# Two-layer encoder trunk: half-width products that take all of k, heads kept in memory, sums on GpSimd

## The chip, the cores and the metric

The kernel runs on one core of one Trainium2 chip. The core's engines are TensorE (PE in the profile: the matrix products; PEld are its weight loads), VectorE (DVE), ScalarE (ACT) and GpSimd (POOL); SyncE (SP) issues most transfers between the chip's memory and SBUF. Each engine works through a list of instructions of its own, in order, and waits at an instruction until what it needs is there. The metric is the device time of one execution in microseconds (us).

## The reference

```python
def reference(x, mem, norm_g, w_in, na_rpb, mem_norm_g, w_mem_kv, w_out, final_g):
    ...
    for l in range(DEPTH):
        h = rms_norm(x, norm_g[l])
        z = h @ w_in[l]
        na_q, na_k, na_v, na_g, dl_q, dl_k, dl_v, dl_g, m_q, m_g = jnp.split(z, offsets, axis=-1)
        ...
        y = jnp.concatenate([o_na * jax.nn.silu(na_g), o_dl * jax.nn.silu(dl_g), o_m * jax.nn.silu(m_g)], axis=-1)
        x = x + y @ w_out[l]
    return rms_norm(x, final_g)
```

Two layers over 512 tokens of 2048 channels in fp32. One projection feeds 16 attention heads of 128 channels (6 neighbourhood, 6 dilated, 4 memory heads) and 16 gates; each head's output times its SiLU gate is one of 16 column tiles of `y`, and a second projection of 16 column tiles is added to `x`.

## The kernel before

Activations lie transposed: a tile has 128 channels on the partitions and 512 tokens along the free side, so `act` (the input of a layer) and `mix` (the gated heads) are 16 tiles each, one for each k tile of the products after them. An fp32 operand is split into a rounded high part and a low remainder (`split`: a ScalarE copy, then a VectorE subtraction), and one product is three matmuls on these parts (`mm3`). Weights come from memory in halves of 8 k tiles (128x1024), are split likewise (`wr` raw, `wh` high, `wl` low; four buffers of each), and `next_half` prepares three halves ahead of the one in use.

A layer runs its value, query and key projections with the attention of each head threaded between them (`steps`, `pump`), then 16 gate columns, then 16 output columns. A plain column (`gemm_t`) is 48 matmuls of 512 tokens. Pairs of columns (`gemm_two`) use a two-by-two scheme of seven products for eight: weights a1, a2 (first column, lower and upper k) and b1, b2 (second column), and tokens cut into a left and a right half of 256. Sums of weights (`combine`, L210 to L213, VectorE) and sums of activations (`whole` and `mix_pair`, L310 to L325, VectorE) are made beside. Before the change a pair takes that scheme on 4 pairs of k tiles, and 8 of the 16 k tiles run plain at 512 tokens (`plain`): 48 matmuls of 512 and 84 of 256. Gate columns 4 to 13 and output columns 2 to 15 (2 to 13 in the second layer, whose last two are done in token halves for the final norm) are such pairs: 23 pairs and 16 plain columns in all.

A head's output stays in SBUF (`o`), and is multiplied by its gate there (L648); the 16 splits of the gated heads (L669) stand between the gates and the output columns. Tiles come from tagged pools, of which the change uses: `u` (63 buffers), `p` (4: scores of a head, old values, sums), `pth` and `ptl` (2 each), `tmp` (4). An instruction that writes a new tile waits until some buffer of its tag is free, that is, until the last reader of an older tile is done. A scheduler sets the order on each engine when the program is built.

Of the kernel before, what the change touches and what calls it, by code (L numbers as in the profile page):

```python
# [9 lines left out]
F32 = mybir.dt.float32  # L10
# [23 lines left out]
U_BUFS = 63  # L34
PAIRS = 4
PLAIN = 2
GATES = range(4, 14)
ASIDE = (2, 3)
# [41 lines left out]
def hybrid_kernel(ctx: ExitStack, tc: tile.TileContext, xT, memT, gains, rpbw, wts, cs_tab, dil_tab, na_tab, outT):  # L80
# [65 lines left out]
    for _ in range(WARM):  # L146
        nc.tensor.matmul(bank[:, :P], lhsT=ones, rhs=ones, start=True, stop=True)
    xs = dpool.tile([KO, P, T], F32, tag="xs", name="xs")


    stream = []
    for layer in range(NL):
        at = 0
        two_by_two = {"o": range(PLAIN, KO if layer + 1 < NL else KO - LAST), "g": GATES}
        for key in SEQ:
            tiles = 4 if key[0] in ("v", "mv") else 1
            if key[1] not in two_by_two.get(key[0], ()):
# [41 lines left out]
    def combine(layer, part, two, at=None):  # L199
# [4 lines left out]
        if part == "raw":  # L204
            a, b, s1 = f32t("wr", W_BUFS, W_HALF), f32t("wr", W_BUFS, W_HALF), tmp()
            two.update(a=a, b=b, s1=s1)
            nc.sync.dma_start(out=a, in_=wts[layer, at, :, :W_HALF])
            nc.sync.dma_start(out=b, in_=wts[layer, at + 1, :, :W_HALF])
# [658 lines left out]
```

## Time and profile before

| | us |
|---|---|
| median of 3 runs (1846.49 to 1846.89) | 1846.72 |
| profiled execution | 1847.28 |
| its span | 1845.5 |
| PE busy in it | 1831.0 (99%) |
| DVE busy | 1086.0 (59%) |
| ACT busy | 751.1 (41%) |
| POOL busy | 53.3 (3%) |

The span runs from the first to the last instruction; the rest of the execution's time lies around it. The granted TensorE clock is 0.998 of full speed (2.4 GHz) over the span. An engine's busy time counts from the start to the end of each instruction, with the time in which another engine holds it up inside it. Neighbouring VectorE instructions overlap a little in the records, so that starts tell better than durations what one costs.

### The profile page before, as it was taken

What the parts mean: (1) busy time and instruction counts of PE and PEld (TensorE: products, weight loads), DVE (VectorE), ACT (ScalarE), POOL (GpSimd) and SP (SyncE); (2) the same over time, 40 slices, a digit from 0 to 9 for tenths busy, and PEclk for the clock granted to TensorE, in tenths of its full rate; (3) what the DMA queues carried; (4) which work ended last, traced back from release to release, by engine and by line L of the source; (5) the groups of instructions that cost most, each with busy time, mean ns of one, the idle gap of its engine ahead of it and who ended that gap; (6) DMA issues with size and microseconds to landing.
All of it is one profiled execution on the core that took longest, in us unless ns stands there. A gap on an engine that the chain in (4) does not pass through costs nothing.

```text
span 1845.5 us, 24250 instructions
## 1 busy us (share of the span) xinstructions
PE 1831.0 (99%) x9586; PEld 1569.0 (85%) x9586; DVE 1086.0 (59%) x1803; ACT 751.1 (41%) x1188; POOL 53.3 (3%) x111
## 2 busy tenths in 40 slices
PE   9999999999999999999999999999999999999997
PEld 8888988888888898899888888888888888988987
DVE  7457553463566866666654564435636658676665
ACT  6346442333334434433443453323333444454442
POOL 0113000100000000000000100000000000000000
PEclk9999999999999999999999999999999999999999
DMA  7335423222222233344643353232222222333433
GB/s 283 102 102 156 137 69 98 89 75 86 86 78 81 79 98 121 123 140 160 183 149 96 112 172 114 70 102 81 69 91 80 78 71 80 104 120 115 132 107 110
DMA packets 69201, 202.99 MB, mean 110 GB/s; under 512 B 7264, under 2 KB 16992, under 8 KB 69088
## 3 DMA queue, kind: packets, MB, share of 16 engines
q1 hardware_dynamic: 68800, 201.16, 34.1%
q8 instruction: 75, 1.23, 0.3%
q10 hardware_dynamic: 288, 0.30, 0.1%
q14 instruction: 38, 0.31, 0.1%
HBM read 193.04 MB, written 8.39 MB: 109 GB/s over the span
## 4 chain that ended last, share of the span: by engine, by line
PE 97%; DVE 1%; DMA 0%; issue 0%; ACT 0%; ACTq 0%; DVEq 0%; SPq 0%
PE acc L247 80%; PE sc L247 10%; PE pv L247 4%; PE sc L418 2%; DVE u L228 0%; DVE wl L222 0%; PE acc L342 0%; DVE wr L761 0%; DMA g_sb<-in_gains 0%; DMA u<-in_memT 0%; PE sc L399 0%; PE sc L746 0%; PE sc L385 0%; DVE p L460 0%; ACT u L227 0%
## 5 line engine op out<-in xcount | busy, mean ns | idle before, releaser
L247 PE MATMUL acc<-u,wh 128*128 128x512 f32 (+1 forms) x3976 | 1113.2, 366 | 0.0
L247 PEld LDWEIGHTS acc<-u,wh 128*128 128x128 f32 x3976 | 706.7, 189 | 107.4
L247 PE MATMUL acc<-u,wl 128*128 128x512 f32 (+1 forms) x1988 | 724.7, 365 | 0.0
L222 DVE TENSOR_TENSOR wl<-wr,wh 128x1024 fp32r<-128x1024 f32 (+1 forms) x344 | 420.8, 1223 | 371.9 <-ACT wh L221 370.6
L221 ACT CAST wh<-wr 128x1024 fp32r<-128x1024 f32 (+1 forms) x344 | 360.6, 1048 | 541.4 <-PE acc L247 436.1
L247 PEld LDWEIGHTS acc<-u,wl 128*128 128x128 f32 x1988 | 375.2, 189 | 61.2
L247 PE MATMUL acc<-wh,u 128*128 128x512 f32 x880 | 283.0, 391 | 0.0
L247 PEld LDWEIGHTS acc<-wh,u 128*128 128x128 f32 x880 | 165.2, 188 | 33.7 <-DVE u L228 0.3
L247 PE MATMUL acc<-wl,u 128*128 128x512 f32 x440 | 171.5, 390 | 0.0
L247 PE MATMUL sc<-u,wh 128*128 128x256 f32 x736 | 138.3, 286 | 0.0
L222 DVE TENSOR_TENSOR ptl<-sc,pth 128x512 fp32r<-128x512 f32 (+2 forms) x112 | 67.5, 603 | 93.6 <-ACT pth L221 93.1
L247 PEld LDWEIGHTS sc<-u,wh 128*128 128x128 f32 x736 | 117.3, 191 | 5.2
L221 ACT CAST pth<-sc 128x512 fp32r<-128x512 f32 (+2 forms) x112 | 57.9, 517 | 123.3 <-PE sc L418 122.7
L247 PE MATMUL sc<-u,wl 128*128 128x256 f32 x368 | 104.1, 283 | 0.0
L247 PEld LDWEIGHTS acc<-wl,u 128*128 128x128 f32 x440 | 82.7, 188 | 16.2
L450 ACT ACTIVATE p<-p,stat 128x256 f32<-128x256 f32 (+1 forms) x96 | 59.2, 616 | 86.9 <-DVE stat L460 86.1
L247 PE MATMUL sc<-u,u 128*128 128x256 f32 (+1 forms) x384 | 80.5, 322 | 0.0
L247 PEld LDWEIGHTS sc<-u,u 128*128 128x128 f32 x384 | 65.3, 188 | 11.6
L247 PEld LDWEIGHTS sc<-u,wl 128*128 128x128 f32 x368 | 70.3, 191 | 0.0
L247 PE MATMUL pv<-pth,u 128*128 128x512 f32 (+2 forms) x224 | 68.4, 386 | 0.0
L221 ACT CAST u<-tmp 128x512 fp32r<-128x512 f32 (+1 forms) x64 | 37.9, 592 | 68.9 <-DVE tmp L580 67.2
L418 PEld LDWEIGHTS sc<-ident,p 128*128 128x128 f32 x376 | 47.8, 140 | 15.2 <-DVE p L453 0.6
(137 smaller groups left out, 1201.0 us busy)
## 6 DMA issues: line engine op xcount, KB each, us to landing
wr<-in_wts SPq DMA_DIRECT2D x319, 512.0 KB, 3.6
p<-in_xT SPq DMA_DIRECT2D x23, 256.0 KB, 4.8
p<-xs SPq DMA_DIRECT2D x22, 256.0 KB, 3.4
u<-in_memT SPq DMA_DIRECT2D x16, 256.0 KB, 4.3
xs<-u SPq DMA_DIRECT2D x16, 256.0 KB, 2.0
outT<-wr SPq DMA_DIRECT2D x6, 512.0 KB, 2.9
e<-in_rpbw SPq DMA_DIRECT2D x12, 192.0 KB, 2.4
pth<-in_xT SPq DMA_DIRECT2D x4, 256.0 KB, 4.9
```

The costliest lines, as they stand in the source:

```text
L221: nc.scalar.copy(hi, x)
L222: nc.vector.tensor_tensor(lo, x, hi.bitcast(F32), ALU.subtract)
L247: nc.tensor.matmul(out, lhsT=a[i], rhs=b[j], start=start and n == 0, stop=stop and n == 2, skip_group_check=shared)
L418: nc.tensor.transpose(tr[:, i * P:(i + 1) * P], probs[qt][:, col:col + P], ident)
L450: nc.scalar.activation(s, src, AF.Exp, bias=neg_max, scale=scale, accum_out=l)
```

## The change

- Pairs of the kind `ns == 8` take the scheme on all 8 pairs of k tiles: seven products of 24 matmuls of 256 tokens, and no plain part. Their weights come as four halves at once (b2, a1, a2, b1), and the four sums s1 = b1 + b2, s3 = b1 + a1, s2 = a1 + s1, s4 = a2 + s2 are made in place, 128x1024 each. Pairs of the kind `ns == 4` keep the old arithmetic.
- Gates: columns 2 to 5 are two pairs of 4, columns 6 to 13 four pairs of 8. Output: columns 2 and 3 a pair of 4, columns 4 to 13 five pairs of 8. In both layers; in all 6 pairs of 4, 18 pairs of 8 and 14 plain columns (the last two of layer two aside, as before).
- Every sum of weights (`add`) and of activations (`mix_pair`) is made by GpSimd. There are 8 sums of activations (`mixed`) for the gates and 8 for the output columns, in place of 4 and 4; each has five GpSimd instructions on 128x256.
- Each head's output goes to memory (`ys`) and is loaded again for its gate; the gated head goes back to `ys`. The splits for the output columns are spread over the last two gate columns (`next_mix`), and the sums for the output columns load their two heads into the two `ptl` buffers (`mix_heads`). Layer two's new columns go to memory (`zs`) and are loaded before the last two columns.
- Tables (mask and rotary) lie in `u` buffers, loaded in each layer; `u` has 66 buffers.

```text
ns == 8, order of the products: b2*mixed[2], a1*left, a2*left, s1*mixed[0], s2*mixed[1], s4*right, s3*mixed[3]
```

```diff
...
-PAIRS = 4
-PLAIN = 2
-GATES = range(4, 14)
-ASIDE = (2, 3)
+U_BUFS = 66
+
+
+GATES_TWO = {2: 4, 4: 4, 6: 8, 8: 8, 10: 8, 12: 8}
+OUT_TWO = {2: 4, 4: 8, 6: 8, 8: 8, 10: 8, 12: 8}
 LAST = 2
...
+        two_by_two = {"g": GATES_TWO, "o": OUT_TWO}
...
+            ns = [two_by_two.get(key[0], {}).get(j) for j in (key[1], key[1] - 1)]
+            if ns[0]:
+
+                two = {"at": at}
+                parts = ("b2", "a1", "a2", "s1", "s2", "s4", "s3") if ns[0] == 8 else (
+                    "first", "a1 a2", "second", "s2 s4", "s1", "s3 b2")
+                stream += [(layer, key, (part, two)) for part in parts]
+            elif not ns[1]:
...
+        def add(out, x, y):
+            nc.gpsimd.tensor_tensor(out, x, y, ALU.add)
...
+        if part in ("first", "second"):
+            return split(load(0 if part == "first" else 1, None, rest), hi, lo)
+        if part == "b2":
+            for name, i, h in (("b2", 1, 1), ("a1", 0, 0), ("a2", 0, 1), ("b1", 1, 0)):
+                two[name] = load(i, h, every)
+        if part == "a1 a2":
+            a, b, s1 = load(0, None, some), load(1, None, some), tmp()
+            two.update({"a1 a2": a, "s2 s4": a, "s3 b2": b, "s1": s1})
...
+            add(s1, b[:, :T], b[:, T:])
+            add(b[:, :T], b[:, :T], a[:, :T])
+            add(a[:, :T], a[:, :T], s1)
+            add(a[:, T:], a[:, T:], a[:, :T])
...
+        w = two[part]
+        n = w.shape[-1]
+        split(w, hi[:, :n], lo[:, :n])
+        if part == "a1":
+            two["s1"], two["s3"], two["s2"] = two["b2"], two["b1"], two["a1"]
+            add(two["s1"], two["b1"], two["b2"])
+            add(two["s3"], two["b1"], two["a1"])
+            add(two["s2"], two["a1"], two["s1"])
+        if part == "a2":
+            two["s4"] = two["a2"]
+            add(two["s4"], two["a2"], two["s2"])
+        return hi, lo
...
-                mm3(acc, (hi[:, sl], lo[:, sl]), act[8 + k8], k8 == 0, False)
+                mm3(acc, (hi[:, sl], lo[:, sl]), act[ns + k8 if k8 < 8 - ns else 8 + k8], k8 == 0, False)
...
-        def product(out, w, c0, b, start=False, stop=False, shared=False):
-            for i in range(PAIRS):
+        def product(out, w, b, start=False, stop=True, c0=0, shared=True):
+            for i in range(ns):
                 sl = slice(c0 + i * P, c0 + (i + 1) * P)
-                mm3(out, (w[0][:, sl], w[1][:, sl]), b(i), start and i == 0, stop and i == PAIRS - 1, shared=shared)
+                mm3(out, (w[0][:, sl], w[1][:, sl]), b(i), start and i == 0, stop and i == ns - 1, shared=shared)
...
+        product(second[:, left], weights(), mixed_of(2), start=True)
+        product(part[:, left], weights(), half_of(0, left), start=True)
         nc.scalar.copy(e1[:, left], part[:, left])
-        product(first[:, left], w, T, half_of(PAIRS, left))
-        plain(second)
-        w = next_half(l, key)
-        product(part[:, left], w, 0, mixed_of(1), stop=True, shared=True)
+        product(first[:, left], weights(), half_of(8, left), start=True)
+        product(part[:, right], weights(), mixed_of(0))
+        product(part[:, left], weights(), mixed_of(1))
         nc.scalar.copy(u2, part[:, left])
-        product(first[:, right], w, T, half_of(PAIRS, right), stop=True)
-        product(part[:, right], next_half(l, key), 0, mixed_of(0), stop=True, shared=True)
         nc.vector.tensor_tensor(e1[:, right], part[:, right], u2, ALU.add)
-        w = next_half(l, key)
-        product(part[:, left], w, 0, mixed_of(3), stop=True, shared=True)
+        product(first[:, right], weights(), half_of(8, right))
+        nc.vector.tensor_tensor(e1, first, e1, ALU.add)
+        product(part[:, left], weights(), mixed_of(3))
         nc.scalar.copy(e2[:, left], part[:, left])
-        nc.vector.tensor_tensor(e2[:, right], part[:, right], e2[:, left], ALU.add)
...
-        return (first, e1, ALU.add), (second, e2, ALU.subtract)
+        nc.vector.scalar_tensor_tensor(e2[:, right], part[:, right], -1.0, e2[:, left], ALU.mult, ALU.subtract)
+        nc.vector.tensor_tensor(e2[:, left], second[:, left], e2[:, left], ALU.subtract)
...
-        nc.vector.tensor_tensor(c[:, :n], y[:, :n], y[:, n:], ALU.subtract)
-        nc.vector.scalar_tensor_tensor(c[:, n:], c[:, :n], -1.0, z[:, n:], ALU.mult, ALU.subtract)
-        nc.vector.tensor_tensor(d[:, n:], z[:, n:], y[:, n:], ALU.subtract)
-        nc.vector.tensor_tensor(d[:, :n], z[:, :n], c[:, n:], ALU.add)
+        for out, a, b, op in ((c[:, n:], y[:, n:], y[:, :n], ALU.subtract), (c[:, n:], c[:, n:], z[:, n:], ALU.subtract),
+                              (c[:, :n], y[:, :n], y[:, n:], ALU.subtract), (d[:, n:], z[:, n:], y[:, n:], ALU.subtract),
+                              (d[:, :n], z[:, :n], c[:, n:], ALU.add)):
+            nc.gpsimd.tensor_tensor(out, a, b, op)
...
                 nc.scalar.copy(out[0], bank[0])
+                nc.scalar.dma_start(out=ys[MIX.index(name)], in_=out[0])
...
+        def head(j, tag="p"):
+
+            y = f32t(tag, 4 if tag == "p" else 2)
+            nc.sync.dma_start(out=y, in_=ys[j])
+            return y
+
+        def gate(j, z, y):
 
             e = tmp()
-            nc.scalar.activation(e, z, AF.Silu)
-            y, = o[MIX[len(gated)]]
-            out = f32t("ptl", 2) if len(gated) in ASIDE else y
-            nc.vector.tensor_tensor(out, y, e, ALU.mult)
-            gated.append(out)
+            nc.vector.tensor_tensor(e, z, rstd, ALU.mult)
+            nc.scalar.activation(e, e, AF.Silu)
+            nc.vector.tensor_tensor(y, y, e, ALU.mult)
+            nc.sync.dma_start(out=ys[j], in_=y)
+
+        def mix_acts():
+            i = len(mixed)
+            if i < 8:
+                mixed.append(mix_pair(whole(act[i]), whole(act[8 + i])))
+
+        todo = list(range(KO - 2))
+
+        def next_mix():
+            for j in todo[:2]:
+                mix[todo.pop(0)] = split(head(j), u32r(), u32r())
 
         for j in range(KO):
-            if j in GATES:
-                if j % 2 == 0:
-                    for acc, e, op in gemm_two(l, ("g", j), act, mixed):
-                        z = f32t("p", 4)
-                        nc.vector.tensor_tensor(z, acc, e, op)
-                        nc.vector.tensor_tensor(z, z, rstd, ALU.mult)
...
-            acc = gemm_t(l, ("g", j), act)
-            z = tmp()
-            nc.vector.tensor_tensor(z, acc, rstd, ALU.mult)
-            gate(z)
-            if j + 2 in (GATES[0], GATES[0] + 1):
-                for i in range(PAIRS // 2 * (j + 2 - GATES[0]), PAIRS // 2 * (j + 3 - GATES[0])):
-                    mixed.append(mix_pair(whole(act[i]), whole(act[PAIRS + i])))
...
-        mix = [split(y, u32r(), u32r()) for y in gated]
...
+            if j in GATES_TWO:
+                y = [head(j), head(j + 1)]
+                for i, z in enumerate(gemm_two(l, ("g", j), act, mixed, GATES_TWO[j], mix_acts)):
+                    gate(j + i, z, y[i])
+            elif j - 1 not in GATES_TWO:
+                last = j >= KO - 2
+                y = head(j, "ptl" if last else "p")
+                gate(j, gemm_t(l, ("g", j), act, beside=next_mix if last else seldom(mix_acts)), y)
+                if last:
+                    mix[j] = split(y, u32r(), u32r())
...
-            if l + 1 < NL:
-                nc.sync.dma_start(out=xs[j], in_=x)
-            else:
+            if l + 1 == NL:
                 nc.scalar.activation(x, x, AF.Copy, scale=g_sb[:, 3 * KO + j:3 * KO + j + 1])
-                out.append(x)
...
+            nc.sync.dma_start(out=(xs if l + 1 < NL else zs)[j], in_=x)
+
+        def mix_heads():
+            i = len(mixed)
+            if i < 8:
+                y, z = f32t("ptl", 2), f32t("ptl", 2)
+                nc.sync.dma_start(out=y, in_=ys[i])
+                nc.sync.dma_start(out=z, in_=ys[8 + i])
+                mixed.append(mix_pair(y, z))
+
+        for j in range(KO if l + 1 < NL else KO - LAST):
+            if j in OUT_TWO:
+                olds = [load_old(j), load_old(j + 1)]
+                for i, x in enumerate(gemm_two(l, ("o", j), mix, mixed, OUT_TWO[j], mix_heads)):
+                    nc.vector.tensor_tensor(olds[i], x, olds[i], ALU.add)
+                    new_x(j + i, olds[i])
+            elif j - 1 not in OUT_TWO:
+                old = load_old(j)
+                acc = gemm_t(l, ("o", j), mix, beside=seldom(mix_heads) if j < KO - 2 else lambda: next_act(l + 1))
+                nc.vector.tensor_tensor(old, acc, old, ALU.add)
...
```

On GpSimd, in the first layer from its last attention head to the gates and beyond: before, the clears of neighbourhood head 5 (`p`) are followed by the mask sums (`nab`) and tables of the second layer.

```order
L477 MEMSET p_3337 128x64
L478 MEMSET p_3337 128x64
L472 TENSOR_TENSOR nab_8666<-e_8664,namask 128x256 x3
L625 TENSOR_TENSOR rope_c<-rope_c,rstd 128x512
L626 TENSOR_TENSOR rope_s<-rope_s,rstd 128x512
```

Now two sums of activations (`p` from `tmp`, made of `act` by VectorE) stand there, then the four weight sums of gate pair 2 (`wr`).

```order
L385 TENSOR_TENSOR p_5014<-tmp_5010 128x256 x2
L385 TENSOR_TENSOR p_5014<-p_5014,tmp_5012 128x256
L385 TENSOR_TENSOR p_5015<-tmp_5012,tmp_5010 128x256
L385 TENSOR_TENSOR p_5015<-tmp_5012,p_5014 128x256
L385 TENSOR_TENSOR p_5075<-tmp_5071 128x256 x2
L385 TENSOR_TENSOR p_5075<-p_5075,tmp_5073 128x256
L385 TENSOR_TENSOR p_5076<-tmp_5073,tmp_5071 128x256
L385 TENSOR_TENSOR p_5076<-tmp_5073,p_5075 128x256
L220 TENSOR_TENSOR tmp_5152<-wr_5150 128x512
L220 TENSOR_TENSOR wr_5150<-wr_5150,wr_5148 128x512
L220 TENSOR_TENSOR wr_5148<-wr_5148,tmp_5152 128x512
L220 TENSOR_TENSOR wr_5148<-wr_5148 128x512
```

What moved: work that VectorE did at the gates stands in GpSimd's list, with sums of activations ahead of the weight sums; six more sums and five more groups of four weight sums follow before the output columns.

On VectorE, at an output pair of the first layer: before, the four weight sums (L210 to L213) lie between the low parts (`wl`) of the weights and the pair's results (`pth`, then `u`).

```order
L210 TENSOR_TENSOR tmp_7090<-wr_7089 128x512
L211 TENSOR_TENSOR wr_7089<-wr_7089,wr_7088 128x512
L222 TENSOR_TENSOR wl_7087<-wr_7088,wh_7086 128x1024
L302 TENSOR_TENSOR pth_6967<-sc_6966,tmp_6969 128x256
L212 TENSOR_TENSOR wr_7088<-wr_7088,tmp_7090 128x512
L222 TENSOR_TENSOR wl_7114<-wr_7112,wh_7113 128x1024
L213 TENSOR_TENSOR wr_7088<-wr_7088 128x512
L306 TENSOR_TENSOR pth_6968<-sc_6966,pth_6968 128x256
L702 TENSOR_TENSOR u_7144<-acc_6964,pth_6967 128x512
L702 TENSOR_TENSOR u_7151<-acc_6965,pth_6968 128x512
L703 TENSOR_TENSOR u_7144<-u_7144,p_6960 128x512
L703 TENSOR_TENSOR u_7151<-u_7151,p_6962 128x512
```

Now, from the end of output pair 4 into pair 6 (results `pth_7432` and `pth_7433` of pair 4; `wl_7619`, `wl_7671`, `wl_7699`, `wl_7728`, `wl_7756` are the low parts of a2, s1, s2, s4, s3 of pair 6):

```order
L359 TENSOR_TENSOR pth_7432<-acc_7429,pth_7432 128x512
L773 TENSOR_TENSOR p_7425<-pth_7432,p_7425 128x512
L253 TENSOR_TENSOR wl_7619<-wr_7554,wh_7618 128x1024
L426 TENSOR_TENSOR ssq<-ssq,tmp_7651 128x512
L253 TENSOR_TENSOR wl_7671<-wr_7550,wh_7670 128x1024
L362 SCALAR_TENSOR_TENSOR pth_7433<-sc_7431,pth_7433 128x256
L363 TENSOR_TENSOR pth_7433<-acc_7430,pth_7433 128x256
L773 TENSOR_TENSOR p_7427<-pth_7433,p_7427 128x512
L253 TENSOR_TENSOR wl_7699<-wr_7552,wh_7698 128x1024
L426 TENSOR_TENSOR ssq<-ssq,tmp_7656 128x512
L253 TENSOR_TENSOR wl_7728<-wr_7554,wh_7727 128x1024
L253 TENSOR_TENSOR wl_7756<-wr_7556,wh_7755 128x1024
```

What moved: the weight sums are gone from VectorE, seven low parts take the place of five and a half, and the old value is added from SBUF to SBUF (L773).

On SP, at the first output columns: before, weights (`wr`), old values (`p`) and results (`xs`) follow each other.

```order
L207 DMA wr_7088<-in_wts 128x1024 [waits DMAHW6_49,DMAHW4_49,DVE_49]
L684 DMA xs<-u_6946 128x512 [waits DMAHW7_49,DVE_49]
L684 DMA xs<-u_6953 128x512 [waits DMAHW0_49,DVE_49]
L678 DMA p_7158<-in_xT 128x512 [waits DMAHW1_49]
L208 DMA wr_7089<-in_wts 128x1024 [waits DMAHW2_49,DVE_49]
L678 DMA p_7160<-in_xT 128x512 [waits DMAHW3_49]
L172 DMA wr_7112<-in_wts 128x1024 [waits DVE_49]
L172 DMA wr_7253<-in_wts 128x1024 [waits DMAHW5_49,DVE_49]
```

Now the heads for the sums of activations (`ptl` from `ys`) stand there, and each waits for GpSimd (Pool) to be done with the head before it; `wr_7308` and `wr_7310` are b2 and a1 of output pair 4.

```order
L719 DMA ys<-ptl_6829 128x512 [waits DMAHW6_49,DVE_49]
L766 DMA ptl_6959<-ys 128x512 [waits DMAHW6_49,DVE_49]
L216 DMA wr_7308<-in_wts 128x1024 [waits DMAHW0_49,DVE_49]
L765 DMA ptl_7007<-ys 128x512 [waits DMAHW3_49,DMAHW1_49,Pool_49]
L766 DMA ptl_7008<-ys 128x512 [waits DMAHW7_49,DMAHW2_49,Pool_49]
L759 DMA xs<-p_6937 128x512 [waits DVE_49]
L752 DMA p_7041<-in_xT 128x512 [waits DMAHW4_49,Activation_49]
L765 DMA ptl_7069<-ys 128x512 [waits DMAHW5_49,DMAHW1_49,Pool_49]
L766 DMA ptl_7070<-ys 128x512 [waits DMAHW2_49,Pool_49]
L765 DMA ptl_7118<-ys 128x512 [waits DMAHW5_49,Pool_49]
L766 DMA ptl_7119<-ys 128x512 [waits DMAHW6_49,DMAHW0_49,Pool_49]
L216 DMA wr_7310<-in_wts 128x1024 [waits DVE_49]
```

What moved: the loads of the heads stand ahead of the weights of pair 4 in the one list, two at a time.

## Rows read from the trace of the kernel before

**Rows 1.** The page: the span, then busy us (share) and instructions of each engine.
```profile
span 1845.5 us, 24250 instructions
...
PE 1831.0 (99%) x9586; PEld 1569.0 (85%) x9586; DVE 1086.0 (59%) x1803; ACT 751.1 (41%) x1188; POOL 53.3 (3%) x111
```

**Rows 2.** Waits of PE: us in total, times, longest.
```profile
PE pv L247 <- DVE ptl L222: 1.1, 3, 0.5
...
PE sc L147 <- POOL ones L124: 1.0, 1, 1.0
```

**Rows 3.** PE in order of time: start us, us, what; one output pair.
```profile
640.06 0.40 PE L247 MATMUL acc<-u,wh 128*128 128x256 f32 x2
...
640.42 0.40 PE L247 MATMUL acc<-u,wh 128*128 128x256 f32 x2
...
643.10 0.63 PE L247 MATMUL acc<-u,wh 128*128 128x512 f32 x2
...
648.57 0.40 PE L247 MATMUL sc<-u,wh 128*128 128x256 f32 x2
...
664.22 0.63 PE L247 MATMUL acc<-u,wh 128*128 128x512 f32 x2
```

**Rows 4.** Stages: us, then busy us (instructions) of the engines; two output pairs.
```profile
622.00:643.10 21.10, 21.10 (x134) 19.10 (x132) 20.13 (x33) 10.12 (x14) 0.00 (x0) 1.00 0.33 100
...
643.10:664.20 21.10, 21.10 (x134) 19.12 (x133) 13.40 (x20) 8.23 (x11) 0.00 (x0) 1.00 0.32 100
```

**Rows 5.** VectorE in order of time, in an output pair.
```profile
791.05 1.22 DVE L222 TENSOR_TENSOR wl<-wr,wh 128x1024 fp32r<-128x1024 f32 x1
...
792.19 0.68 DVE L213 TENSOR_TENSOR wr<-wr 128x512 f32<-128x512 f32 x1
...
792.79 0.42 DVE L306 TENSOR_TENSOR pth<-sc,pth 128x256 f32<-128x256 f32 x1
...
793.12 1.28 DVE L702 TENSOR_TENSOR u<-acc,pth 128x512 f32<-128x512 f32 x2
```

**Rows 6.** GpSimd in order of time, nothing beside it on VectorE ports.
```profile
40.67 2.13 POOL L472 TENSOR_TENSOR nab<-e,namask 128x256 f32<-128x256 f32 x3 [39.19 <-DMA e<-in_rpbw]
...
49.40 1.28 POOL L626 TENSOR_TENSOR rope_s<-rope_s,rstd 128x512 f32<-128x512 f32 x1
```

**Rows 7.** GpSimd and VectorE in order of time where they meet.
```profile
138.75 2.23 POOL L472 TENSOR_TENSOR nab<-e,namask 128x256 f32<-128x256 f32 x3 [2.04 <-DVE stat L460]
...
141.11 2.42 POOL L365 TENSOR_TENSOR macc<-macc,tmp 128x256 f32<-128x256 f32 x2
...
140.31 1.75 DVE L222 TENSOR_TENSOR wl<-wr,wh 128x1024 fp32r<-128x1024 f32 x1
...
141.99 1.83 DVE L228 SCALAR_TENSOR_TENSOR u<-u,g_sb,u 128x256 fp32r<-128x256 f32 x2
...
943.99 1.64 POOL L625 TENSOR_TENSOR rope_c<-rope_c,rstd 128x512 f32<-128x512 f32 x1 [575.39 <-ACT rstd L401]
...
943.26 1.23 DVE L222 TENSOR_TENSOR wl<-wr,wh 128x1024 fp32r<-128x1024 f32 x1 [0.60 <-ACT wh L221]
```

**Rows 8.** Transfers issued: KB each, median us from issue to landing.
```profile
wr<-in_wts SPq DMA_DIRECT2D x319, 512.0 KB, 3.6
...
p<-xs SPq DMA_DIRECT2D x22, 256.0 KB, 3.4
...
e<-in_rpbw SPq DMA_DIRECT2D x12, 192.0 KB, 2.4
```

**Rows 9.** VectorE in order of time, first two gate columns.
```profile
570.41 0.69 DVE L577 SCALAR_TENSOR_TENSOR tmp<-acc,rope_c 128x512 f32<-128x512 f32 x1
...
599.73 0.69 DVE L662 TENSOR_TENSOR tmp<-acc,rstd 128x512 f32<-128x512 f32 x1
```

**Rows 10.** ScalarE groups: busy us, mean ns, idle before.
```profile
L221 ACT CAST wh<-wr 128x1024 fp32r<-128x1024 f32 x342 | 359.4, 1051 | 539.8 <-PE acc L247 436.1 <-issue 66.9 <-PE sc L247 15.4
...
L221 ACT CAST u<-p 128x512 fp32r<-128x512 f32 x32 | 19.2, 617 | 11.9 <-DVE p L322 7.9 <-DVE p L324 4.0
...
L645 ACT ACTIVATE tmp<-p 128x512 f32<-128x512 f32 x20 | 12.4, 633 | 12.1 <-DVE p L657 12.1
```

More of the change, by code (lines that the diff above doesn't have):

```diff
@@ L197, in next_half, with combine, load @@
         return w
-    def combine(layer, part, two, at=None):
+    def combine(layer, part, two):
         hi, lo = f32rt("wh", W_BUFS, W_HALF), f32rt("wl", W_BUFS, W_HALF)
[L204 to L208, printed above, removed]
+        def load(i, h, c):
+            raw = f32t("wr", W_BUFS, W_HALF)
+            src = wts[layer, two["at"] + i].rearrange("p (h c) -> p h c", h=2)
+            if h is None:
+                nc.sync.dma_start(out=raw.rearrange("p (h c) -> p h c", h=2), in_=src[:, :, c])
+            else:
+                nc.sync.dma_start(out=raw, in_=src[:, h, c])
+            return raw
+        def add(out, x, y):
+            nc.gpsimd.tensor_tensor(out, x, y, ALU.add)
+        some, rest, every = slice(0, T), slice(T, W_HALF), slice(0, W_HALF)
+        if part in ("first", "second"):
[6 more added lines that the diff above has]
+            two.update({"a1 a2": a, "s2 s4": a, "s3 b2": b, "s1": s1})
@@ L256, in gemm_t @@
             for k8 in range(8):
+                if beside is not None and k8 % 4 == 0:
+                    beside()
                 ko = half * 8 + k8
@@ L288, in mixed_of @@
                               mixed[i][c // 2][1][:, c % 2 * n:(c % 2 + 1) * n])
[L290 to L293 removed]
+        if ns == 4:
+            plain(first)
+            w = weights()
+            product(part[:, left], w, half_of(0, left), start=True)
+            nc.scalar.copy(e1[:, left], part[:, left])
+            product(first[:, left], w, half_of(8, left), stop=False, c0=T, shared=False)
+            plain(second)
+            w = weights()
+            product(part[:, left], w, mixed_of(1))
+            nc.scalar.copy(u2, part[:, left])
+            product(first[:, right], w, half_of(8, right), c0=T, shared=False)
+            product(part[:, right], weights(), mixed_of(0))
+            nc.vector.tensor_tensor(e1[:, right], part[:, right], u2, ALU.add)
+            nc.vector.tensor_tensor(e1, first, e1, ALU.add)
+            w = weights()
+            product(part[:, left], w, mixed_of(3))
+            nc.scalar.copy(e2[:, left], part[:, left])
+            nc.vector.tensor_tensor(e2[:, right], part[:, right], e2[:, left], ALU.add)
+            product(second[:, left], w, mixed_of(2), c0=T, shared=False)
+            nc.vector.tensor_tensor(e2, second, e2, ALU.subtract)
+            return e1, e2
@@ L310, in whole, with seldom @@
+        return e1, e2
+    def seldom(work):
+        turns = iter(range(100))
+        return lambda: work() if next(turns) % 2 else None
     def whole(x):
@@ L402, in rms_rows, with attend @@
         return pb
-    def attend(q, score, v, order, first, gap, wait):
+    def attend(name, q, score, v, order, first, gap, wait):
         out, probs, pts, bank = [], {}, {}, []
@@ L672, in hybrid_kernel @@
+        assert not steps and not todo
+        mixed = []
+        outs = []
         act = []
-        out = []
-        mixed = []
         def load_old(j):
@@ L712, in hybrid_kernel @@
     olds, ws = {}, {}
+    out = []
+    for j in range(KO - LAST):
+        out.append(u32())
+        nc.sync.dma_start(out=out[j], in_=zs[j])
     for j in cols:
```

100 lines of the change are left out of this document (34 added, 66 removed).

## The prediction

> **What bounds the kernel now.** I read the page first: PE is busy for 1831.0 of the 1845.5 us [rows 1]. The waits of PE come next, since a busy PE can still be a late one; the two longest sums are 1.1 and 1.0 us [rows 2], so nothing makes PE wait, and time can only be saved by giving it fewer or cheaper matmuls. What one costs is read from starts in the timeline: 256 tokens take 0.36/3 = 0.12 us, and 24 of 512 tokens 5.47 us, 0.228 us each [rows 3]. A half-width matmul costs 0.012 us more than half of a full one. A pair of columns takes 664.22 - 643.10 = 21.12 us [rows 3].
>
> PE being the bound says nothing yet of what it would wait for if the rest had more to do. For that I read the stages: in a pair with four sums of activations beside it VectorE is busy 20.13 of 21.10 us, in the next 13.40 [rows 4]. So sums already filled VectorE for a stretch; the other resources stand closer to PE than 59% suggests.
>
> **PE's part.** A pair of the new kind is 168 matmuls of 256: 168 x 0.12 = 20.16 us. A plain column is 48 x 0.228 = 10.94. Before: 23 pairs x 21.12 + 16 columns x 10.94 = 660.8. After: 6 x 21.12 + 18 x 20.16 + 14 x 10.94 = 642.8. PE is given 18.0 us less. The loss is small to begin with: a new pair beats an old one by 0.96 us.
>
> **What VectorE and GpSimd cost, alone and together.** By starts a VectorE instruction costs 1.14 us at 1024, 0.60 at 512 and 0.34 at 256 [rows 5]. GpSimd takes 2.13/3 = 0.71 at 256 and 1.28 at 512 [rows 6]; 0.57 for each 256 more makes 2.42 at 1024, an estimate from these two rows, with 2.3 of it (4 x 0.57) in the data itself.
>
> Together they do not run side by side. A low part of 1024, 1.22 long elsewhere, lasts 1.75 when it starts 0.67 before the third mask sum of GpSimd ends at 140.98; two subtractions of 256 last 1.83 next to two GpSimd sums; and a table product of GpSimd, 1.28 alone, lasts 1.64 while a low part runs until 944.49 [rows 5 to 7]. Each time the later one looks as if it began its work when the earlier one ended, in both directions. I therefore add the GpSimd time to that of VectorE instructions that read two operands in SBUF, and let GpSimd overlap only with VectorE instructions that read PSUM.
>
> The Trainium skill has this as a rule (SBUF — State Buffer, "Who interferes with whom"): a VectorE instruction with two SBUF inputs contends with a GpSimd instruction that reads SBUF, and the second to start blocks until the first is done. By that rule the sums below stand; if it did not hold for GpSimd's wide sums, which no row here shows, the second rival's would.
>
> **Gates: eight sums of activations ahead of the first new pair.** Gate 0 starts near 570.4 and gate 1 ends near 599.7 [rows 9], with the end of the last head's attention in between; two old pairs follow: 29.3 + 2 x 21.12 = 71.5 us to gate pair 6, whose first product takes all eight sums. From the order of the changed VectorE list between the first `whole` and that product: 16 `whole` and 16 low parts of 512 (32 x 0.60 = 19.2), 11 to 14 weight low parts (12.5 to 16.0), 10 more of 512 from SBUF (6.0), so 37.7 to 41.2 on SBUF pairs, and 11.6 that read PSUM or one operand. GpSimd has 40 sums of 256 (40 x 0.57 = 22.8 in the data) and 8 weight sums of 512 (9.1): 31.9. If everything that can overlap does, that is 69.6 us in the 68.5 that are left after the third us, when the first `whole` can start. With no overlap it is 37.7 + 11.6 + 28.4 + 10.2 = 87.9. PE is late by 1 to 19 us, and because the lists are in order, with weight low parts behind those of the sums, it shows already in pairs 2 and 4. Two things lean it upward: the last head's four score tiles, gates 0 and 1 and the sums share four `p` buffers, and each sum passes from VectorE to GpSimd, ScalarE and VectorE. I take 12 per layer.
>
> **Output: sums that load their heads through two buffers.** The load of the next head into a `ptl` buffer waits for the fourth of GpSimd's five instructions, that of its partner for the fifth. From fourth to fourth: landing 3.4 us [rows 8], 0.1 to hand over, then four instructions of 0.71 = 6.3 us. With the 2.4 us in which 192 KB landed it is 5.3. The first sum needs the buffer of gate 15: product, SiLU 0.63, product, copy 0.62 [rows 10], low part, about 4 us into output column 0, then 3.4 for the load and three instructions: 9.6. The eighth ends at 9.6 + 7 x 6.3 = 53.7, with one weight sum of 2.4 ahead of it in GpSimd's list 56.1, split at 57.3. PE wants it at 2 x 10.94 + 21.12 + 2.5 = 45.5 (the eighth k tile in pair 4's first product). So 12 us late, 5 with the short landing. VectorE's SBUF pairs fill about 21 of those 45 us, and 40 GpSimd instructions run into some of them: up to 10 more. I take 15 per layer, between 5 and 22. What waits behind on SP: weights a1, a2 and b1 of pair 4 stand after those loads.
>
> **Each new pair.** On SBUF pairs VectorE has seven low parts (7 x 1.14 = 8.0) and four of 512 (2.4), GpSimd 4 x 2.3 = 9.2: 19.6 of PE's 20.16, 97%. Four other VectorE instructions can overlap. But the chain is longer: all four raw buffers are in use until the low part of s3, the last; only then is b1 of the next pair loaded (3.6 us [rows 8], 3.8 with the hand-over), then come four sums (9.2), and between and behind them, in turn at the ports and in list order, five low parts, a2's to s3's (5.7), and four of 512 (2.4): 21.1 us from low part to low part. That is 0.9 over PE's time, 16 us on 18 pairs. The ends: 0, if VectorE's turns fall into the load's 3.6 us, and 1.8, if its 1.6 on PSUM also lies in the chain (0 to 32 us).
>
> **The rest.** Heads are written on ScalarE's queue and read early enough; the loads hide under the gate columns, and cost nothing as long as their buffers are free. The splits that stood before output column 0 hid under it before (VectorE was the later one only for a stretch) and now under gates 14 and 15: 14 low parts, 8.4 of 21.9 us. At the end 14 columns of 256 KB are read from `zs` ahead of the two old values, while 4 x 48 x 0.12 = 23 us of PE work are left: 0 to 3 us, taken as 1. Below nothing: fewer instructions in the mean on VectorE help no one, as PE never waited for it.
>
> **Sum.** 1847.3 (the profiled execution, 0.6 above the median of the runs and 0.4 above their highest, which is not taken off) - 18.0 + 2 x 12 + 2 x 15 + 16 + 1 = 1900 us. With all low ends 1842, with all high ones 1946.
>
> **Rivals.**
> 1. *Everything stays hidden.* PE's 18.0 us come off: 1829, with a few us of slips 1829 to 1842, faster. For it: PE waited for nothing, VectorE carried four sums in 21.10 us without delay [rows 4], and three halves of lead soften a queue. Against: doubled sums, GpSimd at twice VectorE's price, and the two `ptl` buffers. It decides if ports do not collide and loads of 256 KB land in under 1.9 us (the eighth output sum is then ready at 30.3 + 8 x 1.9 = 45.5).
> 2. *No collisions, only the chain of loads.* VectorE's 49.3 us and GpSimd's 38.6 both fit into the gates' 68.5, and a new pair fits into 20.16. The output sums are still late by 5 to 12 us per layer: 1847.3 - 18.0 + 2 x 12 = 1853, or 1839 with the short landing. Against it: the rows in which either engine held the other.
> 3. *It jams.* Waits of 10 us and more make PE late for its own copies to `part`, sums of the next phase start late, and every new pair stays at 22 us: over 1946. For it: three in-order lists wait for each other; against: only the first products of a phase need all sums.
>
> That the change might not do what it says I exclude: the list of GpSimd has 18 groups of four sums of 1024.
>
> **Chances.** Forecast 0.65 (own range 1862 to 1946), rival 1 0.12, rival 2 0.16 (a quarter of it below 1843), rival 3 0.07. The range 1846 to 1946 leaves out rival 1, the low part of rival 2 and rival 3. About 0.2% (3.7 us) is what a measurement tells from no change: faster 0.14, same 0.05, slower 0.81.
>
> **What would show it.** PE's waits, in each layer: some 15 us before output pair 4, 12 before gate pair 6 or inside gate pairs 2 and 4, and 0.5 to 1.5 us in each new pair, behind weight low parts. GpSimd sums of 1024 well over 2.42 us and low parts of 1024 up to 3.5 where they meet. Matmul steps still 0.12 and 0.228, and a sum of PE time 18 us smaller. I am wrong if low parts stay at 1.22 beside GpSimd's sums, if `ptl` loads follow each other faster than every 5 us, or if PE waits for something not named here. No row of before has PE idle for 10 us, so what such a wait does to its clock is open.

## The result, and the profile after

The changed kernel takes 2029.6 us (median of 4 runs, 2029.4 to 2031.9), the kernel before 1846.7 in the same session: 1.099 times as long, with a 95% interval of 1.097 to 1.101. The forecast was 1900 (1846 to 1946): the direction was right, the size was not. The profiled execution of the changed kernel has a span of 2030.1 us; first its page, to be held against [rows 1].

```profile
span 2030.1 us, 26339 instructions
...
PE 1877.2 (92%) x10270; PEld 1641.1 (81%) x10270; DVE 1255.0 (62%) x1719; ACT 789.9 (39%) x1243; POOL 447.2 (22%) x367
```

PE is idle for 152.9 us, against 14.5 before. And it is *busy* for 46.2 us longer, although it was given less to do. That is its clock: summed over windows of 1 us, busy time x (1 - granted clock) is 60.1 us, against 0.0 before. (The granted clock is the share of full speed that the profile gives.) So PE's work at full clock (busy time less this loss) went from 1831.0 to 1817.1: 13.9 us less, not 18.0. The account of the profiled executions is 1845.5 - 13.9 + 138.4 (idle) + 60.1 (clock) = 2030.1.

What PE waited for (us in total, times, longest), where [rows 2] had 1.1 and 1.0:

```profile
PE sc L278 <- ACT pth L352: 57.1, 17, 4.9
PE sc L278 <- ACT tmp L338: 28.7, 4, 8.1
PE sc L278 <- DVE pth L341: 16.7, 6, 5.4
PE sc L278 <- ACT pth L333: 8.6, 2, 5.8
```

L352, L338 and L333 are ScalarE's copies out of `part`, the PSUM bank in which PE puts several products of a pair one after the other; L341 is VectorE's reading of it. The next product into `part` waits for them. The longest sums are thus not low parts or loads, but small copies of 0.36 us. The stages, layer by layer (us of the window, PE busy, granted clock, DMA share, GB/s): the gates up to pair 4, the gate pairs 6 to 12, four plain columns, output pair 2, output pairs 4 to 12; then one row for the projections and attention of layer 1, and its stages alike.

```profile
575.00:682.00 107.00, 85.52 (x469) 0.94 0.25 84
682.00:783.00 101.00, 86.48 (x631) 0.92 0.49 159
783.00:832.00 49.00, 49.00 (x229) 1.00 0.57 188
832.00:871.00 39.00, 23.02 (x135) 0.74 0.35 108
871.00:995.00 124.00, 107.31 (x806) 0.93 0.47 155
995.00:1570.00 575.00, 575.00 (x2793) 1.00 0.33 110
1570.00:1674.00 104.00, 85.66 (x425) 0.89 0.27 87
1674.00:1775.00 101.00, 87.64 (x662) 0.92 0.43 144
1775.00:1824.00 49.00, 49.00 (x222) 1.00 0.65 203
1824.00:1868.00 44.00, 24.99 (x137) 0.80 0.38 120
1868.00:1995.00 127.00, 109.52 (x833) 0.91 0.45 146
```

Plain columns and attention lose nothing. Window less busy time gives the idle time: 39.8 us in the first gates of both layers, 35.0 around the output pairs 2, 62.0 in the new pairs, where another 31.8 of the 60.1 us of lost clock lie (14.7 and 11.9 in the other two). From VectorE's last sum of one pair to the next, the 18 new pairs take 24.7 us in the mean, and 24 to 27 where the next pair's weight sums run beside them; an old pair took 21.12 [rows 3].

**One new pair.** The rows from the s1 product of output pair 6 to that of pair 8, each engine's in order of time (start, us, engine; in brackets the idle time ahead and who ended it):

```profile
898.17 0.80 PE L278 MATMUL sc<-u,wh 128*128 128x256 f32 x2 [4.88 <-ACT pth L352]
...
907.04 12.01 POOL L220 TENSOR_TENSOR wr<-wr,wr 128x1024 f32<-128x1024 f32 x4 [13.40 <-DMA wr<-in_wts]
...
910.56 3.43 DVE L253 TENSOR_TENSOR wl<-wr,wh 128x1024 fp32r<-128x1024 f32 x1
913.92 2.89 DVE L426 TENSOR_TENSOR ssq<-ssq,tmp 128x512 f32<-128x512 f32 x1
916.73 3.42 DVE L253 TENSOR_TENSOR wl<-wr,wh 128x1024 fp32r<-128x1024 f32 x1
920.07 0.41 DVE L362 SCALAR_TENSOR_TENSOR pth<-sc,pth 128x256 f32<-128x256 f32 x1
...
920.97 0.69 DVE L773 TENSOR_TENSOR p<-pth,p 128x512 f32<-128x512 f32 x1
...
912.27 0.37 ACT L361 COPY pth<-sc 128x256 f32<-128x256 f32 x1
...
921.70 0.63 ACT L424 ACTIVATE tmp<-p 128x512 f32<-128x512 f32 x1 [4.36 <-DVE p L773]
922.23 1.03 ACT L252 CAST wh<-wr 128x1024 fp32r<-128x1024 f32 x1
923.17 0.36 ACT L352 COPY pth<-sc 128x256 f32<-128x256 f32 x1
...
923.58 0.80 PE L278 MATMUL sc<-u,wh 128*128 128x256 f32 x2 [3.60 <-ACT pth L352]
```

This is a loop, and it closes in 923.58 - 898.17 = 25.41 us. PE runs s1 to s3; the last result is copied out at 912.27. Its sum L362 only comes at 920.07, since three VectorE instructions ahead of it, 1.22, 0.68 and 1.22 us elsewhere, last 9.7 us beside GpSimd's four sums of weights for pair 8. Behind L362 comes the new column, then its square on ScalarE, which had waited 4.36 us for it; behind the square, in ScalarE's list, a cast and the copy L352 of the *next* pair, whose a1 product had long been done; and for that copy PE's next s1 product waits. Without the 6.6 us that the three instructions lose, the loop is 18.8 us, shorter than PE's 20.16.

**What the wait does to the clock.** The same place in windows of 2 us:

```profile
918.00:920.00 2.00, 1.98 (x17) 1.00 0.00 0
920.00:922.00 2.00, 0.00 (x0) 0.96 0.31 88
922.00:924.00 2.00, 0.42 (x2) 0.50 0.95 314
924.00:926.00 2.00, 2.00 (x11) 0.50 0.78 244
926.00:928.00 2.00, 2.00 (x11) 0.50 0.86 243
928.00:930.00 2.00, 2.00 (x17) 0.83 0.99 373
930.00:932.00 2.00, 2.00 (x19) 1.00 0.47 182
```

PE stood 3.60 us; then it ran at 0.50 of its clock (the 1.2 GHz level) for some 5 us, 11 matmuls in 2 us instead of 19. The Trainium skill (TensorE: Matmul & The Clock Gate, "HAM oscillation") describes this for a loop that waits for transfers: each wait is paid for again with half a clock after it. This trace agrees, 3.60 us of waiting and then 0.50, with the wait for a copy.

### The profile page after: what moved, and what is told of

It is laid out like the page before. It is cut to its first block, busy times and chain, and to the rows that moved or that the text cites. A ratio compares the mean times of both kernels' runs of the same rounds, so it can differ in the third digit from the quotient of the medians.

```text
span 2030.1 us, 26339 instructions
## 1 busy us (share of the span) xinstructions
PE 1877.2 (92%) x10270; PEld 1641.1 (81%) x10270; DVE 1255.0 (62%) x1719; ACT 789.9 (39%) x1243; POOL 447.2 (22%) x367
## 2 busy tenths in 40 slices
DMA packets 99212, 251.76 MB, mean 124 GB/s; under 512 B 10256, under 2 KB 20240, under 8 KB 99088
## 4 chain that ended last, share of the span: by engine, by line
PE 71%; DVE 11%; issue 6%; POOL 6%; DMA 3%; ACT 2%; POOLq 0%; DVEq 0%; SPq 0%; ACTq 0%
PE acc L278 54%; PE sc L278 11%; POOL p L385 5%; DVE wl L253 4%; PE pv L278 3%; DMA ptl<-ys 2%; PE sc L479 2%; ACT wh L252 1%; POOL wr L220 1%; DVE u L253 1%; DVE ssq L426 1%; DVE p L718 1%; DMA p<-ys 1%; ACT u L252 0%; DVE p L773 0%
## 5 line engine op out<-in xcount | busy, mean ns | idle before, releaser
L278 PE MATMUL acc<-u,wh 128*128 128x512 f32 (+1 forms) x3824 | 1020.4, 355 | 4.0 <-DVE u L253 3.1
L253 DVE TENSOR_TENSOR wl<-wr,wh 128x1024 fp32r<-128x1024 f32 (+1 forms) x381 | 557.6, 1464 | 318.8 <-ACT wh L252 317.4
L278 PE MATMUL acc<-u,wl 128*128 128x512 f32 (+1 forms) x1912 | 676.5, 354 | 0.0
L278 PE MATMUL sc<-u,wh 128*128 128x256 f32 x1344 | 284.8, 312 | 117.0 <-ACT pth L352 57.1
L278 PEld LDWEIGHTS sc<-u,wh 128*128 128x128 f32 x1344 | 240.3, 219 | 125.7 <-ACT pth L352 60.5
L220 POOL TENSOR_TENSOR wr<-wr,wr 128x1024 f32<-128x1024 f32 (+1 forms) x78 | 214.2, 2746 | 238.0 <-DMA wr<-in_wts 167.8
L278 PE MATMUL sc<-u,wl 128*128 128x256 f32 x672 | 206.9, 308 | 0.0
L278 PEld LDWEIGHTS sc<-u,wl 128*128 128x128 f32 x672 | 146.9, 219 | 0.0
L253 DVE TENSOR_TENSOR u<-p,u 128x512 fp32r<-128x512 f32 x92 | 92.7, 1014 | 77.9 <-ACT u L252 76.4
L252 ACT CAST u<-p 128x512 fp32r<-128x512 f32 x92 | 56.4, 620 | 146.2 <-POOL p L385 131.0
```

What stands on the lines that cost most here:

```text
L220: nc.gpsimd.tensor_tensor(out, x, y, ALU.add)
L252: nc.scalar.copy(hi, x)
L253: nc.vector.tensor_tensor(lo, x, hi.bitcast(F32), ALU.subtract)
L278: nc.tensor.matmul(out, lhsT=a[i], rhs=b[j], start=start and n == 0, stop=stop and n == 2, skip_group_check=shared)
```

## Experiments

All are the changed kernel with one edit, unless said otherwise. New pair: mean of the 18. Idle and clock (time lost to it) are PE's in the profiled execution.

| run | us (median) | ratio to before, 95% | new pair | idle | clock |
|---|---|---|---|---|---|
| changed | 2029.6 | 1.097 to 1.101 | 24.7 | 152.9 | 60.1 |
| e1 weight sums on VectorE | 1922.0 | 1.038 to 1.043 | 20.1 | 82.2 | 23.7 |
| e2 activation sums on VectorE | 1963.2 | 1.062 to 1.065 | 24.2 | 108.3 | 32.4 |
| e3 both on VectorE | 1867.9 | 1.009 to 1.014 | 19.8 | 37.5 | 6.2 |
| e4 own bank for s1 | 1980.0 | 1.069 to 1.074 | 21.7 | 122.8 | 35.6 |
| e5 squares on VectorE | 2025.6 | 1.094 to 1.099 | 24.6 | 149.4 | 57.6 |
| e6 heads in `u` | 2018.1 | 1.091 to 1.094 | 24.8 | 147.1 | 51.4 |
| e7 two fills per weight sum | 1909.3 | 1.032 to 1.035 | 20.2 | 72.1 | 18.4 |
| e9 three fills | 1917.8 | 1.037 to 1.040 | 20.6 | 79.3 | 21.1 |
| e10 idle time filled | 2029.0 | 1.097 to 1.101 | 24.5 | 132.5 | 42.3 |

**e1, e2, e3: who adds.**

```
 def add(out, x, y):                      # e1, e3
-    nc.gpsimd.tensor_tensor(out, x, y, ALU.add)
+    nc.vector.tensor_tensor(out, x, y, ALU.add)
 ... in mix_pair                          # e2, e3
-    nc.gpsimd.tensor_tensor(out, a, b, op)
+    nc.vector.tensor_tensor(out, a, b, op)
```

> The changed kernel, but the sums of weights are made by VectorE. Theory A (GpSimd's sums of 1024, 3.0 us each beside VectorE's low parts, hold the low parts of s1 to s3 and everything behind them): new pairs in a row fall from some 25.4 us to 20.2 to 21.0; 14 pairs x 4.4 to 5.2 us, so 1950 to 1968 us in all, with the waits ahead of gate pair 6 and output pair 4 left as they are. Theory B (the late load of b1 is what counts, whoever sums): pairs stay above 24 us, over 2005 us. Theory C (the copy of the a1 product stands too late in ScalarE's list): pairs stay at 23 to 25 us.

> The changed kernel, but the sums of activations (five instructions of 256 each) are made by VectorE. Theory A: pairs in a row keep their 25 to 26 us, only the stretches ahead of the phases' first new pairs get shorter, about 28 us each, four times: up to 110 us less where these waits come from GpSimd's activation sums, 1920 to 1975. Theory D (VectorE has no room for them, as one such sum is then some 4 us of VectorE): 2000 and more.

> The changed kernel with all sums on VectorE, nothing of them on GpSimd. Theory A: nearly all of the loss is gone, 1829 to 1860 us, new pairs 20.2 us. Theory B (chain of loads, two buffers for heads) leaves 10 to 15 us ahead of each output pair 4 and pairs of 24 us: 1950 and more. Theory D (VectorE full): pairs of 21 to 22, 1870 to 1900.

The weight sums on GpSimd cost 108 us, the activation sums 66, both 162. New pairs fall to 20.1 in e1, to PE's own time, so theories B and C, which kept them at 23 or more, fall. e1 came out 28 us below A's range, which left the waits ahead of the first new pairs as they are; in e1 gate pair 4 of layer 0 ends 12.0 us earlier than in the changed kernel. In e2, within A's range, the pairs stay near 24 us, and the waits for L338, 28.7 us in the changed kernel, nearly go:

```profile
PE sc L278 <- ACT pth L352: 48.9, 16, 5.0
...
PE sc L278 <- ACT tmp L338: 3.6, 2, 2.7
```

How the activation sums reached PE shows in output pair 2 of the changed kernel: casts of sums stand in ScalarE's list ahead of the copies, each waiting for GpSimd, and PE goes on only when the copy L338 at 851.21 is through.

```profile
849.22 0.62 ACT L252 CAST u<-p 128x512 fp32r<-128x512 f32 x1 [3.62 <-POOL p L385]
...
851.21 0.36 ACT L338 COPY tmp<-sc 128x256 f32<-128x256 f32 x1
...
851.62 0.80 PE L278 MATMUL sc<-u,wh 128*128 128x256 f32 x2 [7.34 <-ACT tmp L338]
```

e3 is still slower than before, by 21 us and 8 us above A's range: in its profile PE has 12.8 us less work at full clock, but 23.0 more idle time and 6.2 lost to the clock. e3 moves as many bytes as the changed kernel (251.76 MB, against 202.99 before), so the added transfers by themselves can hardly be more than a part of these 21 us. That VectorE is too full to hide all sums fits, but no run shows it by itself.

**e4: the wait comes one product later.**

```
+        mid = sc_bank()
-        product(part[:, right], weights(), mixed_of(0))
+        product(mid[:, right], weights(), mixed_of(0), start=True)
```

(The two later reads of `part[:, right]` go to `mid`.)

> The changed kernel, but the product with s1 goes to a PSUM bank of its own, so that PE reaches the wait for the copy of the a1 product one product (2.88 us) later. Theory C (only the copy's place in ScalarE's list costs): waits for that copy (57 us in all) fall by some 2.9 us each at 17 places and the clock falls less: 1960 to 1985 us. Theory A: the low parts of s1 and s2 come just as late, the wait moves to them and pairs stay at 24 to 25.5 us: 2000 to 2030.

Pairs fall by 3.0 us, about the one product (2.88), although every GpSimd sum is still there, 2.74 us in the median. So the loop does run through the copy, as theory C has it; with e1 it is one chain, not two rivals: the sums make it long, the copy is where it reaches PE. The waits for the copy (L353 here) shrink:

```profile
PE sc L278 <- ACT pth L353: 18.5, 14, 1.9
```

**e5: the square out of ScalarE's list.**

```
+            if on_vector:                # output columns from 4 on
+                nc.vector.tensor_tensor(sq, src, src, ALU.mult)
+            else:
                 nc.scalar.activation(sq, src, AF.Square)
```

> The changed kernel, but in the output columns from 4 on the square of a new column is made by VectorE, so that it no longer stands in ScalarE's list ahead of the copy of the a1 product. Theory C (PE waits for that copy because the square, and behind it the copy, wait for VectorE's sum of the pair before): the output pairs 4 to 10 of layer 0 fall from 25 to 26 us to 21 to 23, those of layer 1 less, as the scaling by the gain stays in the list; gate pairs stay at 25; 2000 to 2018 us. Rival (the low parts themselves are late, the copy only comes last): nothing won, and VectorE has 0.7 us more per column: 2030 to 2045.

A miss for both. Of the four pairs in question of layer 0, two fall to 22.0 and 21.6, the others take 25.0 and 26.4; gate pairs stay. PE's waits for VectorE's read of `part` (L357) grow from 5.9 to 12.3 us: part of the wait moves to another link, behind low parts that are as long as before. The square is one link, not the cause; why only two of the four pairs fall was not found.

**e6: heads through the large pool, not two buffers.**

```
-                y, z = f32t("ptl", 2), f32t("ptl", 2)
+                y, z = u32(), u32()
```

> The changed kernel, but the heads for the output sums are loaded into the large pool's buffers, which are free by then, not through two. Theory P (the prediction's term: a load waits for the fourth GpSimd instruction of the sum before, 6.3 us from sum to sum): the 47 us lost around the two output pairs 2 shrink by 20 to 30, 1998 to 2010 us. Rival G (GpSimd's own 5 x 1.1 us per sum and its weight sums set the pace): at most 10 us less, 2020 to 2030.

11.5 us, between the two ranges and nearer to G: the two buffers are a part of the lateness, and not the larger one.

**e7 and e9: GpSimd busy, but reading nothing.** The weight sums are left out. The one for s3 is put first in the order, so that GpSimd still waits for the load of b1, into whose buffer it writes.

```
-            nc.gpsimd.tensor_tensor(out, x, y, ALU.add)
+            for _ in range(2):               # 3 in e9
+                nc.gpsimd.memset(out, 0.0)
```

> The changed kernel with each of GpSimd's weight sums left out and two fills of its result with zeros in its place, which read nothing in memory; GpSimd is still busy in the same places, and still waits for the load of b1. Theory A, the part on collisions (GpSimd and VectorE shut each other out when both read SBUF): low parts beside the fills last 1.22 us and not 2.9 to 3.4, new pairs 20.2 to 21.5 us, 1920 to 1955 us in all. Rival (it is GpSimd's slowness and the load of b1 that hold the pair, not the collision): low parts short, but pairs of 23 us and more, over 1985 us.

> As the run with fills in place of GpSimd's weight sums (left out), but three fills for each sum, so that GpSimd is busy for 4 x 3 x 0.95 = 11.4 us per pair, nearly the 12.0 of the four sums in the changed kernel. Theory A, collisions: new pairs stay at 20.2 to 20.6 us, 1905 to 1925 us. Rival (the 12 us of GpSimd behind the load of b1 hold the pair whether it reads or not): pairs of 22.5 us and more, over 1940 us.

With two fills (1909.3 us, 11 below A's range) GpSimd works 7.5 us per pair, too few to decide; with three it is 11.1, and the pairs still take 20.6. In e9, where the lines of the helpers are one further down:

```profile
871.61 11.06 POOL L221 MEMSET wr<- 128x1024 f32 x12 [7.65 <-DVE wl L254]
...
873.16 1.23 DVE L254 TENSOR_TENSOR wl<-wr,wh 128x1024 fp32r<-128x1024 f32 x1 [1.61 <-ACT wh L253]
...
876.42 1.22 DVE L254 TENSOR_TENSOR wl<-wr,wh 128x1024 fp32r<-128x1024 f32 x1
877.55 0.68 DVE L427 TENSOR_TENSOR ssq<-ssq,tmp 128x512 f32<-128x512 f32 x1
...
893.81 10.16 POOL L221 MEMSET wr<- 128x1024 f32 x11 [1.09 <-DMA wr<-in_wts]
```

The same instructions that took 3.43 and 2.89 us take 1.22 and 0.68 beside a GpSimd that is nearly as busy (11.06 us against 12.01). So it is not GpSimd's time that holds VectorE, but the sums, which read SBUF where the fills do not; the wait for the load of b1 (the row at 893.81) is still in the kernel, and the pairs stay near PE's own time. The Trainium skill says this (SBUF — State Buffer, "Who interferes with whom"): a VectorE instruction with two SBUF inputs contends with a GpSimd instruction that reads SBUF, not with one that only writes. Both runs agree, with 1.22 us against 3.43.

**e10: the wait filled.**

```
+        spare = sc_bank()               # between the a2 and the s1 product; w: the weights of a2
+        for i in range(5):
+            sl = slice(i * P, (i + 1) * P)
+            mm3(spare[:, left], (w[0][:, sl], w[1][:, sl]), half_of(8, left)(i), i == 0, i == 4)
```

> The changed kernel with 15 additional matmuls of 256 tokens (1.8 us at 0.12) between the a2 and the s1 product of each new pair, into a bank that nobody reads. Theory K (the granted clock falls to half because PE stands idle): in the pairs that wait 3.6 to 5 us there, the 1.8 us lie inside the wait, what stays of it is too short for a fall, the 60 us lost to the clock become 25 to 40, 1995 to 2020 us. Rival (the clock falls for another reason in this stretch): 60 us stay, and the pairs without a wait get 1.8 us longer: 2030 to 2045.

18 x 1.8 = 32.4 us of work were added, and the time stayed. Clock losses fell by 17.8 us, idle time by 20.4. So in sum the clock does follow the idle time, as K says (42.3 is just outside its range), but the time was not won: a pair still lasts 24.5 us, as the loop does not pass through the added work. K's time was wrong, since it left the loop out; why the pairs did not gain what the clock gave back was not found. After a wait of 2.77 us the first two matmuls took 0.80 us, which is half clock; after one of 1.80 they took 0.51, but the clock fell 1.6 us later:

```profile
898.66 0.80 PE L278 MATMUL sc<-u,wh 128*128 128x256 f32 x2 [2.77 <-ACT pth L352]
923.98 0.51 PE L278 MATMUL sc<-u,wh 128*128 128x256 f32 x2 [1.80 <-ACT pth L352]
...
925.00:926.00 1.00, 1.00 (x9) 0.78 0.91 279
926.00:927.00 1.00, 1.00 (x7) 0.50 0.65 174
```

The length of a wait alone does not tell. In the changed kernel two waits of 2.83 us for the same copy were followed by the full clock (gate pair 6 of layer 0) and by half of it (that of layer 1):

```profile
683.89 0.51 PE L278 MATMUL sc<-u,wh 128*128 128x256 f32 x2 [2.83 <-ACT pth L352]
...
1683.62 0.80 PE L278 MATMUL sc<-u,wh 128*128 128x256 f32 x2 [2.83 <-ACT pth L352]
```

**e8, e11, e12: looking for a version that beats both.** All start from e3 and load the heads into `u`.

```
e8   GATES_TWO = {4: 4, 6: 8, 8: 8, 10: 8, 12: 8}
e11  e8, OUT_TWO = {4: 4, 6: 8, 8: 8, 10: 8, 12: 8}, and the edit of e4
e12  e11, 4: 8 in both tables
```

> All sums on VectorE, heads of the output sums loaded into the large pool, and the gates' combined pairs begin with column 4, not 2, two plain columns (2 x 10.94 us) taking the place of one pair of 21.12. The PE part costs 0.76 us more per layer than with all sums on VectorE. Theory A with P: the 29 us of waits and lost clock that were left there fall below 12, 1845 to 1853 us. Rival (the rest is VectorE's own fullness): 1860 to 1872.

> All sums on VectorE, heads of the output sums in the large pool, combined pairs only from column 4 in the gates and in the output, the s1 product in a PSUM bank of its own. PE's part is 13.9 us (measured in the profiles, not the 18.0 of the prediction) less 4 x 0.76 below before: 1835, and what stays of waits is to be under 8 us: 1836 to 1845, faster than before by 0.1 to 0.6%. Rival (VectorE is too full next to the sums of activations): 1850 to 1862, slower than before.

> As the best run so far (all sums on VectorE, heads in the large pool, pairs from column 4, own bank for s1), but the pairs at column 4 take all of k as well: four pairs of 20.16 instead of 21.12, 3.8 us less of PE's work, 1848 to 1850 us, within 0.2% of before. Rival (the eighth sum of a phase is not ready at column 4 and PE waits there 3 us and more, with the clock falling after it): 1855 to 1870.

e8 takes 1870.7 us (1.011 to 1.015 of before), no less than e3, so its theory A falls; e11 1852.6 (1.002 to 1.004), e12 1858.3 (1.006 to 1.009): none beats the kernel before, and all three lie in the ranges of their rivals. In e11 the account is 1845.5 - 11.6 (work) + 14.5 (idle) + 6.2 (clock) = 1854.6: the gain of the new pairs is eaten by waits of up to 4.6 us with their clock. In e12 the four pairs more of the new form were to take 3.8 us off PE's work; at full clock it fell by only 0.7, from 1819.5 to 1818.8, and PE was idle for 30.3 us, against 28.9 in e11. The waits that its rival put at column 4 are there, 0.5 to 2.2 us each.

## Why the prediction was wrong, step by step

- **PE's part, -18.0.** Measured -13.9. The steps 0.12 and 0.228 held, and a new pair that nothing delays takes 20.15 us (e7). The other 4 us lie mostly in single matmul steps that are a little too long, and which busy time hides, since the records of neighbouring matmuls overlap (0.28 us long at steps of 0.12): steps at full clock that are over these two by more than 0.015 us add up to 6.9 us of excess before and 9.3 in the changed kernel (6.4 in e11, 9.2 in e12). The sum had 0.10 of it in each old pair (21.12 against 21.02 by steps) and none in a new one, so it forecast 1.7 us less of it, not 2.4 more. What lengthens these steps was not looked for.
- **The port lock.** Right, in both directions, and shown by e9 for VectorE's side. GpSimd's 1024-wide sum was estimated at 2.42; 2.38 alone, 2.85 in the mean. Low parts were put at up to 3.5 beside it; 3.43 measured. [rows 6] were not quite free of VectorE: beside the mask sums at 40.67 it has three instructions on 4 columns that last 0.66 to 0.70 us instead of 0.16. GpSimd's 0.71 stands all the same, with 0.72 in the changed kernel.
- **Each new pair 21.1 us, 16 us in all.** This is the step that failed: a pair takes 24.7 us, not 21.1. Idle time there is 62.0 us and lost clock 31.8. The prediction followed one chain, from b1's load to the low parts, and asked when the *weights* are ready. The loop that decides goes another way: late low parts, e2's sum behind them, the square or SiLU, and behind that in ScalarE's list the copy out of `part`. It forecast waits "behind weight low parts" of 0.5 to 1.5 us; most were for copies, 17 of 1.1 to 4.9 us.
- **Rival 3, "It jams", had the mechanism** (PE late for its own copies to `part`, three in-order lists that wait for each other) and got 0.07, though it had these begin with waits of 10 us, and the longest was 8.1. What was held against it, that only the first products of a phase need all sums, was true of the sums and not of the copies, which stand in line behind them in every pair.
- **Gates, 24 us.** 39.8 idle and 14.7 of clock. VectorE was forecast full, and in layer 0 the last head's attention waits 7.9 us for it (L514, `ptl` and L521), which fits; but the longest wait, 8.1 us, is for the copy L338, which stood behind casts that waited for GpSimd. Gate pair 4 of layer 0 ends at 680.6 us in the changed kernel, at 668.6 in e1, 662.4 in e2 and 654.0 in e3: both kinds of sums count.
- **Output, 30 us.** 35.0 idle and 11.9 of clock, so the size was nearly right without the clock, the reason mostly not. From VectorE's first reading of gate 15 to its last sum of output pair 2 of layer 0 the changed kernel takes 71.9 us, e6 64.4, e1 67.3, e2 57.4, e3 53.0: the two `ptl` buffers are a part, GpSimd's activation sums the larger one.
- **The clock.** This term failed too: it was put at nothing. "What such a wait does to its clock is open" was written, and 0 was taken; it is 60.1 us, the largest single error.
- **Rivals 1 and 2** fell with the lock: rival 1's 1829 is not reached even with all sums on VectorE.

Of the error of 130 us (2029.6 - 1900), 60 are the clock, 46 the pairs' idle time (62.0 - 16), 21 the first gates and output pairs (74.8 - 54) and 4 PE's work, together 131.

## What to carry to other kernels

Work that was moved from VectorE to GpSimd did not leave VectorE here: each of its instructions in the way lost 2.2 us beside GpSimd's sums. Count such work on both engines, and look at what stands *behind* the lengthened instructions in each in-order list, small copies out of PSUM first. Look for a loop from one iteration to the next, not only for a chain from load to use: PE waited here because the loop (25.4 us) was longer than its own work (20.16), and filling the wait won nothing (e10). And price waits of some us of PE twice, once as idle time and once as clock (138.4 and 60.1 us here).

## What was not expected of the hardware

- Lost clock was 0.4 of the added idle time in the changed kernel (60.1 to 138.4 us). No row of before had shown it, as PE never stood there.
- GpSimd filled 1024 columns in 0.95 us, 0.4 of the 2.38 of a sum, and beside 11 us of such fills VectorE's low parts kept their 1.22 us.
- A sum of squares of 512, 0.68 us alone, lasted 2.89 beside GpSimd's sums: it loses 2.21 us, as much as a low part twice its size (1.22 to 3.43), and nearly what one GpSimd sum takes alone (2.38).
